# A fourth seven-product pair per matrix group, with seven sets of weight sums made during attention and parked in DRAM

## The chip, the cores and the metric

The kernel is one launch on one core of a Trainium2 chip. The metric is device time in microseconds. Before the change it is 1458.26 us (median of three runs, 1458.24 to 1458.92). The core's engines are named as in the profile: PE (matrix products), PEld (its weight loads, which overlap), DVE (elementwise work), ACT (casts, copies, activation functions), POOL (a little elementwise work, and some transfers) and SP (which here only issues transfers).

## The reference

One transformer-like block on x of 256 tokens by 2048. The parts that matter here, cut from the reference:

```
proj = x @ w_in[l]                       # split into q,k,v of two attentions, z, gate_a, gate_b, ...
o_a  = gated_delta_rule_chunked(...)     # a chunked linear attention, with convolution and norm, times silu(z)
o_b  = dsa_sparse_attention(...)         # a top-64 attention
merged = sigmoid(gate_a) * (o_a @ w_branch_a[l]) + sigmoid(gate_b) * (o_b @ w_branch_b[l])
x = layer_norm(ALPHA * x + merged @ w_out[l], ...)
h_gate, h_up = split(x @ w_ffn_in[l], 2)
x = layer_norm(ALPHA * x + (silu(h_gate) * h_up) @ w_ffn_out[l], ...)
```

All inputs are fp32 and the result must be near fp32.

## The kernel before, in words

**Products.** Every fp32 matrix is split into a high part (a cast by ACT, `hi`) and a low part (the difference, by DVE, `lo`). One product is then three matmuls, high by high, high by low and low by high (`mm3`, the lines L210, L211 and L212 of the profile). A chunk of weights is 128 rows by 1024 columns, 512 KB: SP loads it into `raw` (L84), ACT casts it (L86), DVE subtracts (L88).

**Pairs.** A large projection is worked in groups of 1024 columns. The 2048 rows are taken as eight pairs of chunks, q = 0 to 7, and a group adds its eight pairs up in PSUM. A plain pair (`plain_pair`) is eight products, 24 matmuls of 512 columns. A seven-product pair (`seven_pair`) treats the pair as a 2 by 2 block product in Winograd's way: seven products, 21 matmuls. It pays for the missing product with sums: of the weights (`sum13` and `sum24`, DVE, into tiles named `wt`, `f_wt`, `g_wt`), which are split by ACT and DVE too (`thi` and `tlo`), and of x (`x_form`, made once for each q). It also needs four more PSUM banks (`wbank`), which hold the sums that several results share; a short chain (`sums_chain`) adds them up behind the group's last seven-product pair. The two sets of four banks, `acc` and `aux`, change roles from group to group, so `wbank` of one group are the banks that the group before summed its result in, and they are free when DVE has read that result out (L1054 in the gates).

A pair whose weight sums were made ahead (`early_sums`, found in a `ready` table) needs only its first chunk and half of its second one in the usual way. For all others the sums stand right ahead of the pair, among the operations of that pair.

**Which pairs.** The tables GQ (four gate groups), ZQ (z), OQ (output projection) and FQ (ten feed-forward groups) name the pairs that use seven products, and GO and ZO the order of the pairs. Before, most groups have three (2, 4 and 6), the third gate group four.

**Order of work.** PE and SP run in the order in which the program is written. DVE, ACT and POOL are ordered by a scheduler from that program and from priorities. Side work stands in generators (`start`, `tick`): each pair ticks a clock twice, and a generator writes its next piece when its tick comes. So a transfer that such a generator issues on SP stands in SP's list at that place, between the loads of weights.

**Stages**, by the profile of before: first projections, convolution and both attentions (to about 330 us), z, two gate groups for `gate_b`, the product with w_branch_b, two gate groups for `gate_a`, the product with w_branch_a (to about 650), output projection and first layer norm (to about 760), two feed-forward groups in plain form, ten feed-forward groups with pairs (`wfg`, from about 800 to 1227), then the product with w_ffn_out and the last norm. A feed-forward group's result is finished by `hidden_chain`, which among others puts eight transposes (L1337) on PE.

Of the kernel before, what the change touches and what calls it, by code (L numbers as in the profile page):

```python
# [58 lines left out]
def block_kernel(ctx: ExitStack, tc: tile.TileContext, xT, x, cpack, onehot, relb, convw, alog, dtb, gnw,  # L59
# [96 lines left out]
    def join(dst, ps):  # L156
        t = p1.tile([P, S], F32, name="half2", tag="half2", bufs=2)
        nc.scalar.copy(t, ps[:, S:])
        nc.vector.tensor_add(dst, ps[:, :S], t)
# [174 lines left out]
    def T(name, shape, dtype=F32, tag=None):  # L334
        return p1.tile(shape, dtype, name=name, tag=tag or name)
# [140 lines left out]
    def conv_chain(c, pss, ev, dst, c0):  # L476
        pres = []
        for ps in pss:
            pre = p1.tile([P, S], F32, name="pre", tag="pre", bufs=2)
# [431 lines left out]
    for ch in (gates_chain, key_chain, query_chain, value_chain, index_chain, attend_chain, out_gate_chain):  # L911
        start(ch())

    conv_first(s_kT, pss)
    event("kc0")
# [25 lines left out]
    def z_chain():  # L941

        yield "v1"
        yield 1
        t0 = [rp.tile([P, 2, 1024], F32R, name=f"z_t{i}", tag=f"x1_{i}") for i in range(2)]
        wt = two("z_wt", F32, "ol_")
# [36 lines left out]
    def late_form(q):  # L983
        t = T(f"g_form{q}", [P, 2, 4, P], F32R, tag="s_rv")
        gates_form[q] = t[:, 0], t[:, 1]
        room = gates_home["wt"][1][0]
        x_form(q, gates_form[q], room[:, :512], room[:, 512:])

    def ga_chain(src, qs):
        for q in qs:  # L990
            yield from early_sums(src, q, home, ga_ready)
        event("gaready")

# [70 lines left out]
    def merged_chain(j):  # L1064
        yield 1 if j < 3 else 2
        for tb in range(NTB):
            with tc.high_priority(offset=LEAD):
                transposed_split(ga, j, tb)
            yield 1
        if 2 * j in OQ:  # L1070
            yield 1
            room = s_mn.rearrange("p a h d -> p (a h d)")
            x_form(2 * j, gates_form[2 * j], room[:, :512], room[:, 512:1024])
# [8 lines left out]
    def ga_rows():  # L1082
        if "a" not in g_rows:
            for tag in ("thi", "tlo"):
                gates_home[tag] = [0, gates_home[tag][1][:2]]
# [3 lines left out]
    z_ready, ga_ready = {}, {}  # L1089
    start(z_chain())  # L1090
# [12 lines left out]
    late_form(0)  # L1103
    start(ga_chain(wgt[2], (2, 4)))
    for j in range(4):
# [4 lines left out]
    for i in range(2):  # L1110
        gate_group(ga_rows, 2 + i)
    ga = ga_rows()
    need("oa")
    for j in range(4):
# [43 lines left out]

    def load_x():
        for tb in range(NTB):  # L1160
            x1[tb] = rp.tile([P, D], F32, name=f"x1_{tb}", tag=f"x1_{tb}")
            nc.gpsimd.dma_start(x1[tb], x[:, tb, :])

    bank = x_group(woa, OQ, ps_acc, ps_aux, gates_form, home,
                   lambda wbank: seven_chain(0, wbank, mnv.rearrange("p t d -> p (t d)")[:, 1024:1536]), {2: load_x})
    finish()
# [126 lines left out]
    hp2 = fh.enter_context(tc.tile_pool(name="hp2", bufs=1, side="left", reuse_waits="tile"))  # L1293
    for i in (5, 6):
        h_tile(hp2, i)

# [24 lines left out]
    for tb, ps in enumerate(block_xs([wfi[1, k] for k in range(8)], xh, xl)):
        start(h_chain(1, tb, gated(tb, ps), ps_acc))
# [44 lines left out]
    for i in range(1, NG + 1):  # L1367
# [6 lines left out]

        bank = x_group(wfg[i - 1], FQ[i - 1], std, shared, f_form, fhome, lambda wbank: sums_chain(places(), wbank))
        if i == NG:
# [260 lines left out]
```

## Time and profile before

| | |
|---|---|
| median of the runs | 1458.26 us |
| profiled execution | 1458.29 us |
| its span | 1456.5 us |
| PE busy | 1448.7 us (99%) |
| DVE busy | 1241.6 us (85%) |
| ACT busy | 802.6 us (55%) |
| POOL busy | 48.3 us (3%) |
| moved by transfers | 313.32 MB, mean 215 GB/s |
| granted TensorE clock | 1.0 in every stretch |

The span is the profiled execution without 1.8 us around it. Times of the traces below count from the span's start. An engine's busy share is a mean over stages; what a stage has left is read from the windows of that stage.

### The profile page before, as it was taken

What the parts mean: (1) busy time and instruction counts of PE and PEld (TensorE: products, weight loads), DVE (VectorE), ACT (ScalarE), POOL (GpSimd) and SP (SyncE); (2) the same over time, 40 slices, a digit from 0 to 9 for tenths busy, and PEclk for the clock granted to TensorE, in tenths of its full rate; (3) what the DMA queues carried; (4) which work ended last, traced back from release to release, by engine and by line L of the source; (5) the groups of instructions that cost most, each with busy time, mean ns of one, the idle gap of its engine ahead of it and who ended that gap; (6) DMA issues with size and microseconds to landing.
All of it is one profiled execution on the core that took longest, in us unless ns stands there. A gap on an engine that the chain in (4) does not pass through costs nothing.

```text
span 1456.5 us, 19507 instructions
## 1 busy us (share of the span) xinstructions
PE 1448.7 (99%) x7167; PEld 1218.8 (84%) x7167; DVE 1241.6 (85%) x1692; ACT 802.6 (55%) x993; POOL 48.3 (3%) x61
## 2 busy tenths in 40 slices
PE   9999999999999999999999999999999999999998
PEld 8888888888888888888888888888888888888887
DVE  6798985488699958879886899989999998989987
ACT  5765443347466645645535565656566565554552
POOL 0002010020000000000000000000000000000000
PEclk9999999999999999999999999999999999999999
DMA  8646575544556765556856667656666667887853
GB/s 294 195 157 196 178 185 172 172 162 153 174 182 222 239 211 189 192 192 231 296 178 221 227 236 245 210 206 206 228 204 212 216 216 248 310 340 263 330 202 117
DMA packets 94768, 313.32 MB, mean 215 GB/s; under 512 B 16896, under 2 KB 18088, under 8 KB 93904
## 3 DMA queue, kind: packets, MB, share of 16 engines
q1 hardware_dynamic: 83328, 293.25, 59.1%
q0 software_dynamic: 4160, 16.46, 3.6%
q10 hardware_dynamic: 7184, 2.36, 0.7%
q8 instruction: 56, 0.92, 0.2%
q14 instruction: 40, 0.33, 0.1%
HBM read 298.20 MB, written 13.83 MB: 214 GB/s over the span
## 4 chain that ended last, share of the span: by engine, by line
PE 98%; DMA 1%; DVE 0%; ACT 0%; SPq 0%; issue 0%; POOLq 0%; ACTq 0%; DVEq 0%
PE acc L211 11%; PE acc L210 11%; PE acc L212 11%; PE acc L148 10%; PE aux L210 10%; PE aux L212 10%; PE aux L211 10%; PE acc L151 5%; PE acc L168 4%; PE acc L170 4%; PE acc L169 3%; PE aux L168 1%; PE aux L170 1%; PE aux L169 1%; PE aux L723 1%; DMA raw<-in_win_dram 1%
## 5 line engine op out<-in xcount | busy, mean ns | idle before, releaser
L86 ACT CAST hi<-raw 128x1024 fp32r<-128x1024 f32 (+1 forms) x390 | 402.7, 1041 | 367.8 <-PE acc L148 88.2
L88 DVE TENSOR_TENSOR lo<-raw,hi 128x1024 fp32r<-128x1024 f32 (+1 forms) x390 | 470.7, 1216 | 129.2 <-ACT hi L86 126.1
L148 PE MATMUL acc<-X,hi 128*128 128x512 f32 x640 | 203.7, 400 | 0.0
L210 PE MATMUL acc<-hi,X 128*128 128x512 f32 x400 | 156.7, 392 | 0.0
L212 PE MATMUL acc<-hi,X 128*128 128x512 f32 x400 | 155.7, 389 | 0.0
L211 PE MATMUL acc<-lo,X 128*128 128x512 f32 x400 | 155.7, 389 | 0.0
L151 PEld LDWEIGHTS acc<-X,lo 128*128 128x128 f32 x640 | 120.2, 188 | 28.3
L210 PE MATMUL aux<-hi,X 128*128 128x512 f32 x336 | 131.3, 391 | 0.0
L212 PE MATMUL aux<-hi,X 128*128 128x512 f32 x336 | 130.8, 389 | 0.0
L211 PE MATMUL aux<-lo,X 128*128 128x512 f32 x336 | 130.7, 389 | 0.0
L151 PE MATMUL acc<-X,lo 128*128 128x256 f32 x640 | 126.0, 278 | 0.0
L148 PEld LDWEIGHTS acc<-X,hi 128*128 128x128 f32 x640 | 97.5, 189 | 2.0 <-ACT hi L86 0.7
L234 ACT CAST f_thi<-f_wt 128x1024 fp32r<-128x1024 f32 x58 | 61.1, 1053 | 52.4 <-DVE f_wt L244 30.8
L212 PEld LDWEIGHTS acc<-hi,X 128*128 128x128 f32 x400 | 75.1, 188 | 15.7
L210 PEld LDWEIGHTS acc<-hi,X 128*128 128x128 f32 x400 | 75.1, 188 | 15.3 <-ACT s_u L925 0.2
L211 PEld LDWEIGHTS acc<-lo,X 128*128 128x128 f32 x400 | 75.1, 188 | 15.2
L235 DVE TENSOR_TENSOR f_tlo<-f_wt,f_thi 128x1024 fp32r<-128x1024 f32 x58 | 70.2, 1221 | 6.2 <-ACT f_thi L234 6.0
L212 PEld LDWEIGHTS aux<-hi,X 128*128 128x128 f32 x336 | 63.1, 188 | 13.2
L211 PEld LDWEIGHTS aux<-lo,X 128*128 128x128 f32 x336 | 63.1, 188 | 13.0
L210 PEld LDWEIGHTS aux<-hi,X 128*128 128x128 f32 x336 | 63.1, 188 | 12.8
L168 PE MATMUL acc<-hi,X 128*128 128x512 f32 x160 | 64.3, 402 | 0.0
L234 ACT CAST thi<-wt 128x1024 fp32r<-128x1024 f32 x36 | 37.9, 1054 | 45.9 <-DVE wt L239 27.0
(593 smaller groups left out, 2961.5 us busy)
## 6 DMA issues: line engine op xcount, KB each, us to landing
raw<-in_wfg_dram SPq DMA_DIRECT2D x131, 512.0 KB, 4.1
raw<-in_wws_dram SPq DMA_DIRECT2D x80, 512.0 KB, 3.8
raw<-in_wfo_dram SPq DMA_DIRECT2D x70, 512.0 KB, 4.9
raw<-in_wgt_dram SPq DMA_DIRECT2D x51, 512.0 KB, 3.6
f_wraw<-in_wfg_dram SPq DMA_DIRECT2D x29, 512.0 KB, 5.9
raw<-in_win_dram SPq DMA_DIRECT2D x21, 512.0 KB, 3.7
wraw<-in_wfo_dram SPq DMA_DIRECT2D x18, 512.0 KB, 4.9
gt<-d_g SPq DMA_DIRECT2D x18, 512.0 KB, 6.5
```

Source lines behind the costliest of these rows:

```text
L86: nc.scalar.copy(hi, raw)
L88: nc.vector.tensor_sub(lo, raw, hi.bitcast(F32))
L148: nc.tensor.matmul(pss[c], hv[:, kk, cs[c]], X2[k // 4][:, k % 4], start=(k == 0), stop=False, skip_group_check=True)
L151: nc.tensor.matmul(pss[c][:, :S], lv[:, kk, cs[c]], xh[:, k, :], start=False, stop=(k == KT - 1), skip_group_check=True)
L168: nc.tensor.matmul(ps, xh, hv[:, kk], start=(k == 0), stop=False)
L169: nc.tensor.matmul(ps, xh, lv[:, kk], start=False, stop=False)
L170: nc.tensor.matmul(ps, xl, hv[:, kk], start=False, stop=(k == 2 * n - 1))
L210: nc.tensor.matmul(o, sh, hi, start=first, stop=False)
L211: nc.tensor.matmul(o, sh, lo, start=False, stop=False)
L212: nc.tensor.matmul(o, sl, hi, start=False, stop=last)
L234: nc.scalar.copy(hi, v)
L235: nc.vector.tensor_sub(lo, v, hi.bitcast(F32))
```

## The change

Ten pairs of the kind q = 0 become seven-product pairs: in the second and the fourth gate group, in the output projection, and in feed-forward groups 1 to 7.

- For the seven feed-forward groups the weight sums are made by a new generator, `kept_chain`, that starts with the attention generators. For each group it loads the two chunks into one tile (POOL, 1 MB), makes the four sums (DVE, four additions of 512 columns), splits them (ACT two casts, DVE two subtractions of 1024) and writes both parts to a DRAM tensor `d_s` (POOL, twice 1 MB). Its two tiles are those that held the first projection's small weights; z's early sums, which use the same room, are written only after the generator is through (`need("kept")`).
- In the feed-forward stage `kept_load` brings a set back: four SP loads of 512 KB into four tiles. The first set is loaded beside the second plain group, each next one from the pair q = 5 of the group before on. The tiles are single. The pairs run in the order FO, with the kept one fourth.
- In the two gate groups the new pair makes its sums in place, and comes second in the group; before, the first seven-product pair came third.
- In the output projection two pairs (0 and 2) have early sums, made beside the product with w_branch_a, and the order is OO.
- The sums of x for q = 0 (`late_form(0)`) move from behind the second gate group to a generator that is started ahead of the first one. They are made in tiles that attention leaves, and the scheduler puts them near the program's start. `f_forms_chain` makes a set for q = 0 too.
- To make room, the small tiles `half2` and `pre` become pieces of one tile, `load_x` comes in halves, and the space for POOL's transfer descriptors is set to 8192 bytes.

The diff, cut to its core:

```diff
-GQ = ((2, 4, 6), (2, 4, 6), (0, 2, 4, 6), (2, 4, 6))
-GO = (range(8), range(8), (1, 3, 2, 4, 5, 6, 0, 7), range(8))
+GQ = ((2, 4, 6), (0, 2, 4, 6), (0, 2, 4, 6), (0, 2, 4, 6))
+GO = (range(8), (1, 0, 3, 2, 5, 4, 6, 7), (1, 3, 2, 4, 5, 6, 0, 7), (1, 0, 3, 2, 5, 4, 6, 7))
+OO = (1, 3, 0, 2, 5, 4, 6, 7)
-OQ = (2, 4, 6)
+OQ = (0, 2, 4, 6)
-FQ = ((4, 6), *[(2, 4, 6)] * 9)
+KEPT = 7
+FQ = ((0, 4, 6), *[(0, 2, 4, 6)] * (KEPT - 1), *[(2, 4, 6)] * (10 - KEPT))
+FO = (1, 3, 2, 0, 4, 5, 6, 7)
...
+    d_s = dr.tile([KEPT, 2, P, 2, 1024], F32, name="d_s")
+    def kept_chain():
+        raw, hi = T("k_raw", [P, 2, 1024], tag="oh_"), T("k_hi", [P, 2, 1024], F32R, tag="ol_")
+        (r0, r1), (s0, s1) = ([raw[:, i, n * 512:n * 512 + 512] for n in range(2)] for i in range(2))
+        for m in range(KEPT):
+            nc.gpsimd.dma_start(raw, wfg[m, 0:2].rearrange("k p c -> p k c"))
+            yield 3
+            nc.vector.tensor_add(r0, r0, s1)
+            nc.vector.tensor_add(s1, r1, s1)
+            yield 1
+            nc.vector.tensor_add(r1, r0, r1)
+            nc.vector.tensor_add(s0, r1, s0)
+            yield 1
+            for i in range(2):
+                nc.scalar.copy(hi[:, i], raw[:, i])
+                nc.vector.tensor_sub(raw[:, i].bitcast(F32R), raw[:, i], hi[:, i].bitcast(F32))
+                yield 1
+            nc.gpsimd.dma_start(d_s[m, 0], hi.bitcast(F32))
+            nc.gpsimd.dma_start(d_s[m, 1], raw)
+            yield 4
+        event("kept")
...
+    def kept_load(m):
+        for i in range(2):
+            if m:
+                kept[i] = [hp2.tile([P, 1024], F32R, name="kept", tag=f"{hl}{5 + i}") for hl in ("hH", "hL")]
+            for j in range(2):
+                nc.sync.dma_start(kept[i][j].bitcast(F32), d_s[m, j, :, i])
+                yield 2
...
+        k_ready[0] = t1, t2, t3, t4
...
+        at = {5: lambda i=i: start(kept_load(i))} if i < KEPT else {}
+        bank = x_group(wfg[i - 1], FQ[i - 1], std, shared, f_form, fhome, lambda wbank: sums_chain(places(), wbank),
+                       at, FO, k_ready)
```

**Where instructions move: SP in the feed-forward groups.** One steady group of SP's list before, in which `f_wraw` with the `raw` behind it are the two loads of a seven-product pair, here of q = 2, 4 and 6:

```order
L273 DMA f_wraw<-in_wfg_dram 128x1024
L275 DMA raw<-in_wfg_dram 128x1024
L84 DMA raw<-in_wfg_dram 128x1024 x2
L273 DMA f_wraw<-in_wfg_dram 128x1024
L275 DMA raw<-in_wfg_dram 128x1024
L84 DMA raw<-in_wfg_dram 128x1024 x2
L273 DMA f_wraw<-in_wfg_dram 128x1024
L275 DMA raw<-in_wfg_dram 128x1024
L84 DMA raw<-in_wfg_dram 128x1024 x6
```

The same place after the change, from the pair q = 4 on:

```order
L276 DMA f_wraw<-in_wfg_dram 128x1024
L278 DMA raw<-in_wfg_dram 128x1024
L87 DMA raw<-in_wfg_dram 128x1024 x2
L1373 DMA kept<-d_s 128x1024
L276 DMA f_wraw<-in_wfg_dram 128x1024
L278 DMA raw<-in_wfg_dram 128x1024
L1373 DMA kept<-d_s 128x1024
L87 DMA raw<-in_wfg_dram 128x1024 x2
L1373 DMA kept<-d_s 128x1024
L87 DMA raw<-in_wfg_dram 128x1024 x2
L1373 DMA kept<-d_s 128x1024
```

The first of the four `kept` loads stands ahead of the two loads of q = 6, and waits until PE has read the tile's present contents, which it does in the group's own fourth pair.

**DVE from the first to the second gate group.** Before (L1008 to L1013 add up the shared banks of the first group, L1054 read its result out, the rest prepares the second group's pairs):

```order
L1008 TENSOR_TENSOR gb_4291<-gb_4291,acc 128x512
L1009 TENSOR_TENSOR gb_4290<-acc,gb_4291 128x512
L1012 TENSOR_TENSOR gb_4291<-gb_4291,acc 128x512
L1013 TENSOR_TENSOR gb_4291<-acc,gb_4291 128x512
L1054 TENSOR_TENSOR gb_4290<-aux,gb_4290 128x512
L88 TENSOR_TENSOR lo<-raw,hi 128x1024
L239 TENSOR_TENSOR g_wt<-g_wraw,raw 128x1024
L1054 TENSOR_TENSOR gb_4290<-aux,gb_4290 128x512
L243 TENSOR_TENSOR g_wt<-g_wt,g_wraw 128x512
```

and now (L1049 to L1054 are the former L1008 to L1013, L1095 the former L1054):

```order
L1049 TENSOR_TENSOR gb_4322<-gb_4322,acc 128x512
L242 TENSOR_TENSOR g_wt<-g_wraw,raw 128x1024
L1050 TENSOR_TENSOR gb_4321<-acc,gb_4322 128x512
L246 TENSOR_TENSOR g_wt<-g_wt,g_wraw 128x512
L1053 TENSOR_TENSOR gb_4322<-gb_4322,acc 128x512
L247 TENSOR_TENSOR g_wt<-g_wt,raw 128x512
L1054 TENSOR_TENSOR gb_4322<-acc,gb_4322 128x512
L238 TENSOR_TENSOR lo<-g_wraw,hi 128x1024
L238 TENSOR_TENSOR lo<-raw,hi 128x512
L238 TENSOR_TENSOR g_tlo<-g_wt,g_thi 128x1024 x2
L1095 TENSOR_TENSOR gb_4321<-aux,gb_4321 128x512
L91 TENSOR_TENSOR lo<-raw,hi 128x1024
```

The sums and splits of the second group's first seven-product pair now stand ahead of all four reads of the first group's result. Before, one read stood ahead of them, one among them, and two followed them (further down, not shown).

More of the change, by code (lines that the diff above doesn't have):

```diff
@@ L156, in join @@
     def join(dst, ps):
-        t = p1.tile([P, S], F32, name="half2", tag="half2", bufs=2)
+        t = pieces(1)
         nc.scalar.copy(t, ps[:, S:])
@@ L347, in block_kernel, with pieces @@
     s_sq = T("s_sq", [P, 1024])
+    s_pc = T("s_pc", [P, 1024])
+    T("s_x", [P, 2048])
+    turns = [0, 0]
+    def pieces(i):
+        turns[i] += 1
+        return s_pc[:, (2 * i + turns[i] % 2) * S:(2 * i + turns[i] % 2 + 1) * S]
     first_ = [T(n, [P, H * S], F32R, tag=t) for n, t in (("wsh", "oh_"), ("wsl", "ol_"))]
@@ L478, in conv_chain @@
         for ps in pss:
-            pre = p1.tile([P, S], F32, name="pre", tag="pre", bufs=2)
+            pre = pieces(0)
             join(pre, ps)
@@ L912, in block_kernel @@
         start(ch())
+    d_s = dr.tile([KEPT, 2, P, 2, 1024], F32, name="d_s")
[19 more added lines that the diff above has]
+        event("kept")
+    start(kept_chain())
     conv_first(s_kT, pss)
@@ L944, in z_chain @@
         yield 1
+        need("kept")
         t0 = [rp.tile([P, 2, 1024], F32R, name=f"z_t{i}", tag=f"x1_{i}") for i in range(2)]
@@ L983, in late_form, with early_chain, next_sets @@
     def late_form(q):
-        t = T(f"g_form{q}", [P, 2, 4, P], F32R, tag="s_rv")
+        t = T(f"g_form{q}", [P, 2, 4, P], F32R, tag="s_pc")
         gates_form[q] = t[:, 0], t[:, 1]
-        room = gates_home["wt"][1][0]
+        yield 3
+        room = T("f_room", [P, 1024], tag="s_x")
         x_form(q, gates_form[q], room[:, :512], room[:, 512:])
-    def ga_chain(src, qs):
+    def early_chain(src, qs, ready, ev):
         for q in qs:
-            yield from early_sums(src, q, home, ga_ready)
-        event("gaready")
+            yield from early_sums(src, q, home, ready)
+        event(ev)
+    def next_sets(*olds):
+        for tag, old in zip(("thi", "tlo"), olds):
+            e = gates_home[tag]
+            gates_home[tag] = [0, e[1][:2] + halves(two("h_" + old, F32R, old))[1]]
     def x_form(q, dst, x32, g):
@@ L1071, in merged_chain @@
             yield 1
-            room = s_mn.rearrange("p a h d -> p (a h d)")
+            room = wo_room
             x_form(2 * j, gates_form[2 * j], room[:, :512], room[:, 512:1024])
@@ L1097, in block_kernel @@
     gates_buffers()
+    start(late_form(0))
     for i in range(2):
@@ L1102, in block_kernel @@
         gates_home[tag][0] = 0
-    late_form(0)
-    start(ga_chain(wgt[2], (2, 4)))
+    start(early_chain(wgt[2], (2, 4), ga_ready, "gaready"))
     for j in range(4):
@@ L1112, in block_kernel @@
     ga = ga_rows()
+    next_sets("s_x", "s_rv")
+    wo_room = T("wo_room", [P, 2048], tag="s_mn")
+    start(early_chain(woa, (0, 2), wo_ready, "woready"))
     need("oa")
@@ L1293, in block_kernel @@
     hp2 = fh.enter_context(tc.tile_pool(name="hp2", bufs=1, side="left", reuse_waits="tile"))
-    for i in (5, 6):
-        h_tile(hp2, i)
+    kept = [[hp2.tile([P, 1024], F32R, name="kept", tag=f"{hl}{i}") for hl in ("hH", "hL")] for i in (5, 6)]
     f_home = {}
@@ L1318, in f_forms_chain @@
             x_form(q, f_form[q], fv(), fv())
+    k_ready = {}
+    def kept_load(m):
[5 more added lines that the diff above has]
+                yield 2
+        (t1, t2), (t4, t3) = ([tuple(t[:, n * 512:n * 512 + 512] for t in kept[i]) for n in range(2)]
+                              for i in range(2))
+        k_ready[0] = t1, t2, t3, t4
     start(f_forms_chain())
+    start(kept_load(0))
     for tb, ps in enumerate(block_xs([wfi[1, k] for k in range(8)], xh, xl)):
@@ L1373, in places @@
             return sums
-        bank = x_group(wfg[i - 1], FQ[i - 1], std, shared, f_form, fhome, lambda wbank: sums_chain(places(), wbank))
+        at = {5: lambda i=i: start(kept_load(i))} if i < KEPT else {}
+        bank = x_group(wfg[i - 1], FQ[i - 1], std, shared, f_form, fhome, lambda wbank: sums_chain(places(), wbank),
+                       at, FO, k_ready)
+        if i == KEPT:
+            for k in (5, 6):
+                h_tile(hp2, k)
         if i == NG:
```

20 lines of the change are left out of this document (11 added, 9 removed).

## The prediction

> **What bounds the kernel now.** I read the page's busy times and chain first, then what PE waited for, then the windows of DVE stage by stage.
>
> ```profile
> span 1456.5 us, 19507 instructions
> PE 1448.7 (99%) x7167; PEld 1218.8 (84%) x7167; DVE 1241.6 (85%) x1692; ACT 802.6 (55%) x993; POOL 48.3 (3%) x61
> PE 98%; DMA 1%; DVE 0%; ACT 0%; SPq 0%; issue 0%; POOLq 0%; ACTq 0%; DVEq 0%
> PE aux L407 <- DVE warm L403: 1.1, 1, 1.1
> PE acc L134 <- DVE lo L88: 1.1, 3, 0.6
> ```
>
> PE is busy for 99% of the span and makes 98% of the chain. Its two largest waits are 1.1 us each, both at the start. So time goes down only by matmuls that disappear, and comes back only as new waits of PE. The next two questions are what a matmul is worth, and how much room DVE has where it gets more to do.
>
> ```profile
> 858.63 0.39 PE L210 MATMUL aux<-hi,X 128*128 128x512 f32 x1
> 860.90 0.39 PE L211 MATMUL aux<-f_tlo,f_form 128*128 128x512 f32 x1
> ...
> 80.00:94.00 14.00, 14.00 (x89) 12.50 (x88) 14.00 (x27) 11.29 (x15) 0.77 (x3) 1.00 0.47 144
> 94.00:108.00 14.00, 14.00 (x91) 12.56 (x90) 13.74 (x57) 8.76 (x12) 0.20 (x1) 1.00 0.49 160
> 108.00:122.00 14.00, 14.00 (x85) 12.34 (x84) 10.97 (x23) 7.63 (x11) 5.08 (x2) 1.00 0.68 169
> 122.00:136.00 14.00, 14.00 (x82) 12.20 (x81) 11.04 (x31) 9.17 (x14) 0.16 (x1) 1.00 0.63 227
> ...
> 443.00:464.00 21.00, 21.00 (x94) 17.41 (x93) 20.07 (x23) 14.75 (x18) 0.00 (x0) 1.00 0.71 239
> 464.00:485.00 21.00, 21.00 (x94) 17.38 (x94) 18.43 (x24) 11.48 (x15) 0.00 (x0) 1.00 0.59 190
> 590.00:611.00 21.00, 21.00 (x95) 17.38 (x94) 17.41 (x19) 11.18 (x13) 0.00 (x0) 1.00 0.57 179
> 674.00:695.00 21.00, 21.00 (x94) 17.41 (x93) 20.93 (x27) 12.64 (x15) 0.00 (x0) 1.00 0.72 258
> 989.00:1010.00 21.00, 21.00 (x94) 17.41 (x93) 18.34 (x23) 11.19 (x13) 0.00 (x0) 1.00 0.72 237
> 1010.00:1031.00 21.00, 21.00 (x99) 17.47 (x98) 21.00 (x27) 14.26 (x19) 0.53 (x1) 1.00 0.52 184
> ```
>
> From the first to the last of the two matmuls there are ten steps in 2.27 us, so 0.227 us each, though each shows 0.39: they overlap. In the windows the third busy figure is DVE's. DVE has no idle time left at 80 to 94 us (14.00 of 14), about 3.5 of 42 us in the second gate group, and 2.7 of 42 in a feed-forward group.
>
> **What is removed.** Ten pairs go from 24 to 21 matmuls: 30 x 0.227 = 6.8 us. Nothing lies over these, so if PE waits no more than before, the profiled execution of 1458.29 becomes 1451.5. Everything below is what PE may wait for again.
>
> **The kept sums beside attention.** For DVE and ACT the prices are these:
>
> ```profile
> L88 DVE TENSOR_TENSOR lo<-raw,hi 128x1024 fp32r<-128x1024 f32 x381 | 464.5, 1228 | 124.4 <-ACT hi L86 121.4
> L235 DVE TENSOR_TENSOR lo<-raw,hi 128x512 fp32r<-128x512 f32 x62 | 42.5, 686 | 0.0
> 107.55 1.22 DVE L88 TENSOR_TENSOR lo<-raw,hi 128x1024 fp32r<-128x1024 f32 x1
> 113.72 0.39 PE L151 MATMUL acc<-X,lo 128*128 128x256 f32 x2
> 124.66 1.22 DVE L88 TENSOR_TENSOR lo<-raw,hi 128x1024 fp32r<-128x1024 f32 x1
> 128.53 0.39 PE L151 MATMUL acc<-X,lo 128*128 128x256 f32 x2
> x<-in_x_dram POOLq DMA_DIRECT2D x2, 1024.0 KB, 7.9
> ```
>
> Back to back the 1024 form takes about 1.13 us and the 512 form 0.60 (starts in the feed-forward rows below), so a set is 4 x 0.60 + 2 x 1.13 = 4.7 us of DVE, seven sets 33 us. Most of it lies in attention's idle DVE time. It doesn't where DVE is full: the second set's work falls at about 73 to 91 us by its place among neighbours that exist in both programs. The window ahead still takes some of it; I carry about 3.5 us of lateness past 94, and DVE is idle for 0.26 until 108 and 3.0 until 122. The low part made at 107.55 ends at 108.77 and is used at 113.72: 4.95 us of room, less the 3.5 and what of the third set comes before it, so 0 to 0.5 lost. The one at 124.66 ends at 125.88 and is used at 128.53, 2.65 of room, against about 3.5 - 3.0 left plus the third set's pieces in that place: 0 to 1.5. The other places have more room. POOL adds a chain of its own: it holds back each next load until the last set's writes have landed, and attention's reciprocal roots wait behind that in its queue. The seven sets lie between about 35 and 260 us, some 30 us apart, and a 1 MB transfer of POOL's landed after 7.9 us (the last row), so I count on cover there: write, load and 4.7 us of sums fit; without it, the next set's first sum holds DVE, in order, for as long as the load is late. In all 0 to 3; I take **0.6**, nearer the covered end because all but two of the places have over 3 us.
>
> x_form(0) near the start is five small operations more among the first chunks (0.69 + 4 x 0.29 = 1.9 us at most), next to PE's start-up waits of 1.1: 0 to 0.3, taken 0.1. It leaves the stage behind the second gate group, where DVE had no idle time, which helps there.
>
> **Gates and output projection.** A pair that makes its own sums costs DVE 1.13 + 1.13 + 0.60 + 1.13 + 2 x 0.60 + 1.13 = 6.3 us against 2.3 for a plain one: 4 more in each of two gate groups. The fourth has 3.6 idle in its middle half and more behind; the second about 3.5 of its 42, less 0.7 by which it shrinks. And its shared banks are wanted 5.44 us earlier:
>
> ```profile
> 439.40 0.68 DVE L1008 TENSOR_TENSOR gb<-gb,acc 128x512 f32<-128x512 f32 x1
> 442.72 0.69 DVE L1054 TENSOR_TENSOR gb<-aux,gb 128x512 f32<-128x512 f32 x1 [0.33 <-PE aux L212]
> 445.44 1.23 DVE L239 TENSOR_TENSOR g_wt<-g_wraw,raw 128x1024 f32<-128x1024 f32 x1 [0.89 <-DMA raw<-in_wgt_dram]
> 438.38 0.33 SPq L275 DMA_DIRECT2D raw<-in_wgt_dram  x1
> 444.56 0.39 PE L210 MATMUL acc<-hi,X 128*128 128x512 f32 x1
> 455.44 0.39 PE L210 MATMUL aux<-hi,X 128*128 128x512 f32 x1
> 567.83 0.69 DVE L1008 TENSOR_TENSOR ga<-ga,aux 128x512 f32<-128x512 f32 x1 [0.83 <-ACT ga L1006]
> ```
>
> The group begins at 444.56, the first shared bank was wanted at 455.44 and is now at 450.0, the fourth 2.0 later. I walk DVE's new list from 439.40: the sum can start at 440.3 if its rows have landed (their buffer comes free around 435.5 instead of 438), and seven operations up to the fourth bank's sum end at 444.4, two 1024 splits, a 512 and another 1024 at 448.4; the first read ends at 449.0, the fourth, with a low part between, at 451.9 (wanted by 453.4). Room about 1 us everywhere. The same walk from the last row's place, where the idle 0.83 takes most of the first sum, leaves the fourth group 0.6 to 1.3. So 0 if loads are on time; a load as late as the one above (7.1 us from 438.38 to 445.44) would cost about 1.5 in each group. With the lateness carried into the product behind the second group, 0 to 3; taken **0.3**. In the output projection the two early pairs take work out of a full stage (20.93 of 21) and the first shared bank is wanted third as before: 0.
>
> **Feed-forward: the kept loads on SP.** DVE gets 0.5 us less per group, so its share is no issue. What changes is SP's list. Before, the loads of q = 6 ran far ahead:
>
> ```profile
> 974.94 0.43 SPq L273 DMA_DIRECT2D f_wraw<-in_wfg_dram  x1
> 978.57 0.33 SPq L275 DMA_DIRECT2D raw<-in_wfg_dram  x1
> 986.82 1.22 DVE L239 TENSOR_TENSOR f_wt<-f_wraw,raw 128x1024 f32<-128x1024 f32 x1
> 994.44 1.23 DVE L235 TENSOR_TENSOR f_tlo<-f_wt,f_thi 128x1024 fp32r<-128x1024 f32 x1 [1.20 <-ACT f_thi L234]
> 996.02 0.39 PE L210 MATMUL acc<-hi,X 128*128 128x512 f32 x1
> 999.64 0.39 PE L211 MATMUL acc<-f_tlo,f_form 128*128 128x512 f32 x1
> f_wraw<-in_wfg_dram SPq DMA_DIRECT2D x29, 512.0 KB, 5.9
> raw<-in_wfg_dram SPq DMA_DIRECT2D x131, 512.0 KB, 4.1
> ```
>
> Call the start of q = 6 on PE Q (996.02 here). The two loads were issued at Q - 21.1 and Q - 17.5, the sum made at Q - 9.2, and the last low part, which ends at 995.67, was ready 4.0 us before its use at Q + 3.6. Now the `kept` load ahead of them waits for the end of the fourth pair, q = 0, which lies before q = 4 (4.76), q = 5 (5.44) and q = 6: Q - 10.4. So f_wraw goes out at about Q - 10.1 and raw at Q - 9.7; SP stands still for about 11 us, with the loads of q = 6, q = 7 and the next group's first pairs behind it. With 5.2 us for the one and 6.4 for the other in such a burst they land at Q - 4.9 and Q - 3.3. Then DVE, which has waited some 5 us: low part to Q - 2.7, sum to -1.6, 512 low part -1.0, half sum -0.4, low part of the first sum 0.8 (wanted at 2.3), half sum 1.4, one low part of q = 7 2.5, low part of the second sum 3.7, wanted at 3.6. That is just enough. With the medians' 4.1 us for raw, 2.2 of room; with the 7.1 of the gates' load, 0.8 lost. Six groups have such a load: 0 to 4.8, taken 0.2 each, **1.2**. DVE comes out about 3.7 us late of that place and meets little idle time afterwards (2.7 per group), so the transposes' inputs and the next second pair lose up to 1 now and then: **0.3**, with 0 to 2.
>
> [...]
>
> The traffic that the loads add, 2 MB less 0.25 per 41.7 us, is some 42 GB/s on 184 to 237, and is covered:
>
> ```profile
> 1346.00:1367.00 21.00, 21.00 (x95) 17.38 (x94) 20.27 (x22) 12.29 (x14) 2.08 (x4) 1.00 0.97 354
> ```
>
> Here 354 GB/s moved and PE stayed busy for 21.00 of 21. The small descriptor space, the halves of load_x and the moved tiles I take at 0; POOL has 97% of its time free.
>
> **Sum.** 1458.29 - 6.8 + 0.6 + 0.1 + 0.3 + 1.2 + 0.3 = 1454.0. The profiled execution is 0.03 above the median, which changes nothing.
>
> **Rivals.**
> - *Nothing waits:* 1451.5 to 1452.2. For it: the walks end with room, if small; against it: four places with 1 us or less.
> - *The kept load starves q = 6.* One mechanism, SP's standstill, decides alone. Each us by which `raw` lands after Q - 3.2 costs PE one us in each of six groups. At 1.1 us (landing 7.5 after its issue) the gain is all but gone with the other terms: 1458.6, no change. Slower than 1461.2 takes 1.6 or more, a landing at 8 us: the four transfers, q = 7's and POOL's would have to share. At 9 us it is 1458.29 - 6.8 + 1.3 + 6 x 2.6 = 1468. For it: the burst of six loads after 11 us of silence and the 7.1 above; against it: the 5.9 median, in the same stage.
> - *DVE in attention:* the sets come late, by POOL's chain or by lateness that adds up over the full windows, and PE waits once for each set in three or four places, 1 to 1.5 us each: 1454.0 - 0.6 + 4 to 5 = 1457.4 to 1458.4, no change.
>
> [...]
>
> **Chances.** A change of 0.2% (2.9 us) is about what can be told here. The sum as worked out, 1452.2 to 1455.3: 0.48. Nothing waits: 0.14. Standstill to no change 0.18, to slower 0.10. Attention 0.10, no change. Together faster 0.62, no change 0.28, slower 0.10. I predict 1454.0, with 1452.2 to 1456 as its own range; eight in ten lie within 1451.4 to 1459.0.
>
> **What would show it.** In the profile after: PE busy near 1442 and its waits, by releaser. If I am right, PE's waits grow by 1 to 4 us, the most on L235's successor (f_tlo, L238) once per feed-forward group, and f_wraw of q = 6 goes out about 10 us before its pair, right behind a kept load. DVE's idle time before sum13 (`f_wt`) grows by about 5 us in six groups, released by a transfer. If PE waits for lo (L91) between 105 and 135 us, attention was underrated. If PE waits on L1095 at 448 to 454 or 576 to 582, the gates were. The forecast is wrong if PE's waits exceed 5 us in all, or if the kept loads' standstill isn't there.

## The result and the profile after

The changed kernel takes 1479.44 us (median of four runs, 1477.17 to 1482.98). The kernel before, run beside it, takes 1458.25 (four runs, 1457.68 to 1458.92). The ratio is 1.0146, with a 95% interval of 1.0133 to 1.0158: slower by 21 us, where 1454.0 was forecast and 1459.0 was the end of the range.

The page of the changed kernel, its span, busy times and chain:

```profile
span 1478.1 us, 19641 instructions
PE 1454.1 (98%) x7137; PEld 1217.4 (82%) x7137; DVE 1281.3 (87%) x1761; ACT 818.8 (55%) x1019; POOL 63.8 (4%) x84
PE 74%; DVE 13%; DMA 8%; issue 3%; ACT 2%; SPq 0%; POOLq 0%; ACTq 0%; DVEq 0%
```

PE does 30 matmuls fewer (7137 for 7167), but it is no longer the whole chain: 98% has become 74%, and 21% lies on DVE and transfers. The list of what PE waited for (us in total, times, longest):

```profile
PE acc L154 <- DVE lo L91: 5.9, 4, 2.8
PE aux L613 <- ACT s_t L619: 3.1, 1, 3.1
PE aux L214 <- DVE h_s_rv L238: 1.5, 1, 1.5
PE aux L214 <- DVE f_tlo L238: 1.5, 3, 0.8
PE acc L214 <- DVE f_tlo L238: 1.3, 2, 0.8
...
PE aux L213 <- DVE v L1054: 0.8, 1, 0.8
```

L154 and L613 stand in attention, h_s_rv in the output projection, f_tlo and v in the feed-forward stage. Over all of the program PE's waits come to 19.5 us, against 3.5 before. To put a price on each place, I matched every matmul of a changed kernel to the same matmul of the kernel before and subtracted the times. The differences by stage, for the changed kernel and for four experiments told below (worked out from the profiled executions; minus is gained; each row holds what was gained or lost within that stage; "late load" is the kept load one pair later, "two tiles" the second form of that experiment):

```
us gained or lost in           changed  work only  late load  two tiles  four groups
start (to 60 us)                 +1.2     -0.1       -0.2       +0.7        +0.3
attention, 60 to 136             +9.6     +1.1       +9.8        0.0         0.0
attention, 136 to 206            +1.2     +0.3       +1.0        0.0         0.0
attention, 206 to 262            +6.6     +0.4       +3.7       +7.4        +0.6
262 to 440                        0.0     +0.2        0.0       +0.2        +0.3
two gate groups                  -1.4     -1.4       -1.3       -1.3        -1.3
output projection                +1.9     +2.0       +2.1       -0.7        -0.6
feed-forward groups              +2.5     +2.8       -4.8       -4.8        -2.7
```

A group whose new pair costs nothing else gains 0.68: 3 matmuls of 0.227. The gates show just that, twice. The changed kernel loses 17.4 in attention, 2.5 around the gain of 0.7 in the projection, and 7.3 around the gain of 4.8 (7 x 0.68) in the feed-forward groups.

**Attention, first place.** DVE's timeline at the second set (start, duration, operation; L932 is a set's first sum, L564 attention's own; the bracket is the idle time before an instruction and what ended it), then POOL's (L943 writes a set's low part, L930 loads the next set):

```profile
79.92 0.69 DVE L932 TENSOR_TENSOR k_raw<-k_raw 128x512 f32<-128x512 f32 x1 [6.78 <-DMA k_raw<-in_wfg_dram]
...
84.98 1.28 DVE L564 TENSOR_TENSOR s_e<-aux,gc 128x512 f32<-128x512 f32 x2
```

```profile
62.86 0.55 POOL L943 DMA_DIRECT2D d_s<-k_raw  x1 [4.23 <-DVE k_raw L940]
69.64 0.72 POOL L930 DMA_DIRECT2D k_raw<-in_wfg_dram  x1 [6.23 <-DMA d_s<-k_raw]
```

POOL can load the second set into the one tile only when the first set's write has landed, 6.2 us after POOL itself was free. The load then takes 10.3 us, from 69.64 to 79.92. DVE reached the first sum at 73.1 and stood there 6.78 us, with attention's own work behind it. Nothing of it shows on PE at once: PE has work until 89, and then waits for a low part at 90.90, 108.77 and 123.01. Three transfers were in flight together: in the windows from 62 to 68 us the DMA engines were busy all the time (1.01 to 1.04), and up to 76 for nine tenths of it or more (0.90 to 1.02). In the load's last 4 us they were not (0.68 of 76 to 78, 0.15 of 78 to 80); why it still had not landed is not shown.

```profile
64.00:66.00 2.00, 2.00 (x13) 1.76 (x12) 0.51 (x1) 1.99 (x4) 0.00 (x0) 1.00 1.02 422
...
74.00:76.00 2.00, 2.00 (x13) 1.77 (x12) 0.00 (x0) 1.90 (x5) 0.00 (x0) 1.00 0.97 322
```

The columns are the stretch, its length, busy times of PE, PEld, DVE, ACT and POOL, the granted clock, the DMA engines' busy share and GB/s. From 74 to 76 DVE does nothing. Afterwards it has no slack in which to catch up: from 80 to 124 us it waits only once more, for 0.9 us, and PE's three waits fall in this stretch.

The same stall of DVE costs nothing elsewhere. The seventh set's first sum waits too, 5.76 us, and PE stays full:

```profile
272.41 0.69 DVE L932 TENSOR_TENSOR k_raw<-k_raw 128x512 f32<-128x512 f32 x1 [5.76 <-DMA k_raw<-in_wfg_dram]
```

```profile
262.00:270.00 8.00, 8.00 (x70) 6.94 (x70) 2.45 (x2) 3.28 (x4) 0.72 (x1) 1.00 0.91 325
270.00:278.00 8.00, 8.00 (x53) 6.80 (x51) 5.45 (x9) 1.84 (x4) 0.00 (x0) 1.00 0.19 57
```

There DVE is busy for only 7.9 of 16 us; at 80 to 94 the kernel before had no idle time on it at all (14.00 of 14 in the prediction's windows).

**Attention, second place.** A piece of the chain, then POOL's timeline (s_bm is a gather of many small rows, eight transfers that attention needs):

```profile
228.76 12.06 DMA raw<-in_wws_dram
240.92 1.04 ACT hi L89
241.97 0.38 ACT s_t L619
```

```profile
212.61 0.53 POOL L943 DMA_DIRECT2D d_s<-k_raw  x1 [7.55 <-DVE sc L811]
219.80 0.71 POOL L930 DMA_DIRECT2D k_raw<-in_wfg_dram  x1 [6.66 <-DMA d_s<-k_raw]
220.50 3.73 POOL L825 DMA_DIRECT2D s_bm<-d_tab  x7
```

Here it is a weight load of SP's that is late: 12 us after its issue, where such loads took 3.8 in the median before. On ACT the small copy s_t stands behind that load's cast (240.92, then 241.97), so it is late too, and PE waits 3.1 us for it. Beside the load, POOL moves a 1 MB set and the gather; from 226 to 242 us the DMA engines were busy all the time (1.01 to 1.05 in windows of 4 us).

**Output projection.** POOL's x loads, SP's load of the early pair's second chunk, and DVE's sum:

```profile
686.72 1.17 POOL L1207 DMA_DIRECT2D x<-in_x_dram  x2 [337.22 <-PE aux L1102]
688.12 0.33 SPq L278 DMA_DIRECT2D raw<-in_woa_dram  x1
696.18 1.22 DVE L242 TENSOR_TENSOR g_wt<-g_wraw,raw 128x1024 f32<-128x1024 f32 x1 [4.52 <-DMA raw<-in_woa_dram]
```

The load lands 8 us after its issue and DVE stands for 4.5, ahead of two pairs with early sums; PE waits at 709.76 and 714.98.

**Feed-forward.** SP's timeline around a kept load, and DVE's up to the late low part:

```profile
920.55 0.33 SPq L1373 DMA_DIRECT2D kept<-d_s  x1
920.93 0.43 SPq L276 DMA_DIRECT2D f_wraw<-in_wfg_dram  x1
```

```profile
928.63 1.22 DVE L242 TENSOR_TENSOR f_wt<-f_wraw,raw 128x1024 f32<-128x1024 f32 x1
931.05 1.23 DVE L238 TENSOR_TENSOR f_tlo<-f_wt,f_thi 128x1024 fp32r<-128x1024 f32 x1
933.47 1.23 DVE L91 TENSOR_TENSOR lo<-raw,hi 128x1024 fp32r<-128x1024 f32 x1 [0.59 <-ACT hi L89]
934.61 1.22 DVE L238 TENSOR_TENSOR f_tlo<-f_wt,f_thi 128x1024 fp32r<-128x1024 f32 x1
```

```profile
935.88 0.50 PE L214 MATMUL acc<-f_tlo,f_form 128*128 128x512 f32 x1 [0.84 <-DVE f_tlo L238]
```

This is the standstill of the forecast, in its place and order. The idle time it makes stands on ACT, as its wait for f_wraw:

```profile
ACT hi L237 <- DMA f_wraw<-in_wfg_dram: 31.6, 6, 6.5
```

### The profile page after: what moved, and what is told of

The parts are those of the page before. It is cut to its first block, busy times and chain, and to the rows that moved or that the text cites. A ratio compares the mean times of both kernels' runs of the same rounds, so it can differ in the third digit from the quotient of the medians.

```text
span 1478.1 us, 19641 instructions
## 1 busy us (share of the span) xinstructions
PE 1454.1 (98%) x7137; PEld 1217.4 (82%) x7137; DVE 1281.3 (87%) x1761; ACT 818.8 (55%) x1019; POOL 63.8 (4%) x84
## 4 chain that ended last, share of the span: by engine, by line
PE 74%; DVE 13%; DMA 8%; issue 3%; ACT 2%; SPq 0%; POOLq 0%; ACTq 0%; DVEq 0%
PE acc L214 9%; PE acc L215 9%; PE acc L213 8%; PE aux L214 8%; PE aux L215 8%; PE aux L213 8%; PE acc L151 4%; PE acc L173 3%; PE acc L171 3%; PE acc L172 3%; DVE lo L91 3%; DMA raw<-in_wws_dram 2%; PE acc L154 2%; DMA f_wraw<-in_wfg_dram 1%; PE aux L171 1%
## 5 line engine op out<-in xcount | busy, mean ns | idle before, releaser
L89 ACT CAST hi<-raw 128x1024 fp32r<-128x1024 f32 (+1 forms) x388 | 396.0, 1031 | 338.8 <-PE acc L215 68.6
L91 DVE TENSOR_TENSOR lo<-raw,hi 128x1024 fp32r<-128x1024 f32 (+1 forms) x388 | 462.6, 1203 | 95.8 <-ACT hi L89 94.0
L154 PEld LDWEIGHTS acc<-X,lo 128*128 128x128 f32 x640 | 121.4, 191 | 37.5 <-DVE lo L91 9.3
L213 PE MATMUL acc<-hi,X 128*128 128x512 f32 x370 | 145.2, 392 | 0.0
L215 PE MATMUL acc<-hi,X 128*128 128x512 f32 x370 | 144.2, 390 | 0.0
L214 PE MATMUL acc<-lo,X 128*128 128x512 f32 x370 | 144.0, 389 | 0.0
L154 PE MATMUL acc<-X,lo 128*128 128x256 f32 x640 | 128.5, 283 | 6.0 <-DVE lo L91 5.9
L213 PE MATMUL aux<-hi,X 128*128 128x512 f32 x306 | 119.8, 392 | 1.1 <-DVE v L1054 0.8
L214 PE MATMUL aux<-lo,X 128*128 128x512 f32 x306 | 119.2, 390 | 0.4 <-DVE lo L238 0.4
L215 PE MATMUL aux<-hi,X 128*128 128x512 f32 x306 | 119.2, 389 | 0.0
L215 PEld LDWEIGHTS acc<-hi,X 128*128 128x128 f32 x370 | 69.5, 188 | 14.7
L213 PEld LDWEIGHTS acc<-hi,X 128*128 128x128 f32 x370 | 69.5, 188 | 14.1 <-ACT s_u L959 0.2
L214 PEld LDWEIGHTS acc<-lo,X 128*128 128x128 f32 x370 | 69.5, 188 | 14.1
L238 DVE TENSOR_TENSOR f_tlo<-f_wt,f_thi 128x1024 fp32r<-128x1024 f32 x58 | 70.4, 1220 | 1.7 <-ACT f_thi L237 1.5
L213 PEld LDWEIGHTS aux<-hi,X 128*128 128x128 f32 x306 | 57.4, 188 | 13.6 <-DVE v L1054 1.2
L214 PEld LDWEIGHTS aux<-lo,X 128*128 128x128 f32 x306 | 57.5, 188 | 12.5 <-DVE lo L238 0.9
L215 PEld LDWEIGHTS aux<-hi,X 128*128 128x128 f32 x306 | 57.4, 188 | 12.0
L171 PE MATMUL acc<-hi,X 128*128 128x512 f32 x160 | 64.3, 402 | 0.0
```

The costliest lines, as they stand in the source:

```text
L89: nc.scalar.copy(hi, raw)
L91: nc.vector.tensor_sub(lo, raw, hi.bitcast(F32))
L154: nc.tensor.matmul(pss[c][:, :S], lv[:, kk, cs[c]], xh[:, k, :], start=False, stop=(k == KT - 1), skip_group_check=True)
L171: nc.tensor.matmul(ps, xh, hv[:, kk], start=(k == 0), stop=False)
L213: nc.tensor.matmul(o, sh, hi, start=first, stop=False)
L214: nc.tensor.matmul(o, sh, lo, start=False, stop=False)
```

## The experiments

My first theory after the result had three independent parts: in attention DVE, in order, is held by a load that came late (and not by its own 33 us of work); in the projection the x loads collide with the early pair's loads; in the feed-forward stage the kept load stands ahead of q = 6's loads in SP's list. Rivals: DVE's added work itself; the added transfers as such.

**Gates and projection alone.** No sums made ahead, the feed-forward groups as before:

```diff
-KEPT = 7
+KEPT = 0
-    start(kept_chain())
-    start(kept_load(0))
```

> Only the gates and the output projection have their fourth pair; nothing is made beside attention or kept, and the feed-forward groups are as before. If the changed kernel's ledger by stage adds up (start +1.1, attention +17.5, gates -1.4, output projection -0.7 +2.5, feed-forward -4.8 +7.3), this gives 1458.25 + 1.1 - 1.4 - 0.7 + 2.5 = 1459.8. If the output projection's 2.5 us are an echo of the lateness that attention left, they are gone and it gives 1457.3.

Measured 1459.22 (ten runs) beside 1458.49: ratio 1.0004 [0.9994, 1.0014], the first of the two forecasts: the projection's loss is no echo of attention's. The gates gain 0.68 each; the projection gives 2.3 back around its 0.68, and PE's largest wait is the 1.5 us for h_s_rv, as in the changed kernel.

**The same with x loaded by SP**, late in the stage, instead of by POOL beside the early pair's loads:

```diff
-            nc.gpsimd.dma_start(x1[tb][:, cs], x[:, tb, cs])
+            nc.sync.dma_start(x1[tb][:, cs], x[:, tb, cs])
-                   ... {0: load_x}, OO, wo_ready)
+                   ... {7: load_x}, OO, wo_ready)
```

> As x1_gates_proj, with x loaded by SP behind the last non-ready seven-product pair. If POOL's x loads beside the early pairs made PE wait in the output projection, the 2.3 us lost there fall to 0.3 or less: 1456.4 to 1457.0. If DVE's order in that stage did, they stay: 1459.

Measured 1456.55 (ten runs, 1455.16 to 1460.32) beside 1458.08: ratio 0.999 [0.9981, 1.0000]. The wait for h_s_rv is gone and the projection gains a clean 0.68. So what the projection lost hung on the place and queue of the x loads, not on the early pairs' work; which of the two, place or queue, was not separated.

**The chain's transfers alone:** each set is loaded and written back, without sums and splits.

> The chain beside attention only loads and writes; the sums, casts and subtractions are left out (what is kept is then the plain weights). If late weight loads cost the time (SP's loads share the engines with POOL's), attention still loses 10 us or more: 1472 to 1479. If DVE's work costs it, or DVE's standstill at the sums' load, attention loses 3 at most: 1461 to 1465.

Measured 1474.83 (one run); 13.9 us lost in attention. It looks like a verdict for the transfers, but it does not separate them from POOL's order. Nothing paced POOL any more, its transfers ran back to back, and two small pieces of attention's own work were queued behind them: a reciprocal root (`rk`), which POOL did at 119.14 in the changed kernel, and the clearing of a tile (s_e, L679 on POOL), for which DVE then stood 9.96 us:

```profile
124.20 0.55 POOL L935 DMA_DIRECT2D d_s<-k_raw  x1 [10.02 <-DMA k_raw<-in_wfg_dram]
...
125.40 3.20 POOL L473 TENSOR_TENSOR rk<-ssk,half 128x16 f32<-128x16 f32 x1
143.31 0.16 DVE L682 TENSOR_TENSOR s_e<-s_e 128x2 f32<-128x2 f32 x1 [9.96 <-POOL s_e L679]
```

Nearly all of its loss lies between 114 and 136 us (in the times of the kernel before). What follows is only that a wait of POOL's can cost as much by this other way.

**The chain's work alone:** all sums and splits stay, but only the first set is loaded and written, so later sets wait for nothing.

```diff
-            nc.gpsimd.dma_start(raw, wfg[m, 0:2].rearrange("k p c -> p k c"))
+            if not m:
+                nc.gpsimd.dma_start(raw, wfg[m, 0:2].rearrange("k p c -> p k c"))
```

> The chain beside attention does all of its sums, casts and subtractions, but only the first of the seven sets is loaded and written; the others work on what lies there, and the feed-forward groups all read the first set. If DVE's work costs the time, attention still loses 14 us or more: 1475 or more. If the transfers do it, as late weight loads or as DVE's standstill at the sums' load, it loses 1 to 4: 1461 to 1466.

Measured 1463.63 (one run). Attention loses 1.8 in place of 17.4. DVE's rows at the second set (the lines stand one further down here, so L933 is a set's first sum):

```profile
71.81 0.68 DVE L933 TENSOR_TENSOR k_raw<-k_raw 128x512 f32<-128x512 f32 x1
...
77.80 1.29 DVE L564 TENSOR_TENSOR s_e<-aux,gc 128x512 f32<-128x512 f32 x2 [0.26 <-PE aux L563]
```

The sum starts without a wait, and attention's L564 at 77.80 in place of 84.98. So DVE's work for seven sets costs at most 1.8 us; the forecast's price for it was right. This run takes away the transfers and the standstill together; which of the two counts is left to the run with two tiles. The projection and the feed-forward stage lose as in the changed kernel.

**Kept load one pair later,** behind the loads of q = 6 in SP's list; the rest is the changed kernel:

```diff
-        at = {5: lambda i=i: start(kept_load(i))} if i < KEPT else {}
+        at = {6: lambda i=i: start(kept_load(i))} if i < KEPT else {}
```

> As the changed kernel, but each kept load starts one pair later, so that it stands behind the two loads of q = 6 in SP's list. If SP's standstill ahead of these loads makes the 7.3 us lost in the feed-forward groups, 5 of them or more are gone, and f_wraw of q = 6 goes out 15 us or more before its pair: about 1473 to 1475. If the kept bytes themselves (2 MB more per group) make them, the loss stays: 1478 to 1481.

Measured 1468.93 (one run), below the 1473 to 1475 expected. The feed-forward groups gain 4.75, which is 7 x 0.68: nothing is lost any more. No f_tlo and no v is left among PE's larger waits:

```profile
PE acc L154 <- DVE lo L91: 6.5, 4, 4.7
PE aux L613 <- ACT s_t L619: 1.5, 1, 1.5
PE aux L214 <- DVE h_s_rv L238: 1.5, 1, 1.5
```

So the place in SP's list was the whole cause there, with the waits for v as a consequence. Attention still loses 14.5. That is 2.9 less than in the changed kernel, and the start costs 1.4 less, though the edit touches neither; the changed kernel's own four runs spread over 5.8 us, so single runs are read here by stage and for differences larger than that of a stage left alone.

**Two set tiles.** With the late kept load and x by SP, each set is loaded a set ahead, into a second tile (that of `s_x`). Its first use must wait until s_x's old content is done with. In the first form I made that wait with a small copy on DVE that reads the first set:

```diff
+        nc.vector.tensor_copy(s_x[:, :1], raws[0][:, 0, :1])
+        raws.append(T("k_raw", [P, 2, 1024], tag="s_x"))
...
+            if m + 1 < KEPT:
+                load(m + 1)
             nc.vector.tensor_add(r0, r0, s1)
```

> All seven sets beside attention, with the later kept load of x4_late_load, x loaded by SP behind the last non-ready seven-product pair of the output projection instead of by POOL, and a second tile for the chain's load: each set is loaded a whole set ahead, so that DVE's sums need not wait for a load and the load not for the last set's writes. Bytes and DVE work are the same. If DVE's standstill at k_raw (13.9 us in the changed kernel) costs attention its time, its loss falls from 14.3 to 5 or less: 1453 to 1458. If the transfers themselves, which make SP's weight loads late, cost it, the loss stays at 9 or more: 1462 to 1467. In the output projection the 2.5 us should go, if POOL's x loads made the pair's second load late.

Measured 1464.07 (one run), and the copy had the very fault that it was to cure:

```profile
46.37 0.15 DVE L934 COPY s_x<-k_raw 128x1 f32<-128x1 f32 x1 [6.25 <-DMA k_raw<-in_wfg_dram]
```

DVE stood 6.25 us for it, and 4.8 us were lost at about 50 to 62. This repeats the mechanism in another place. Another 8.4 us followed up to 262, so the loss did not fall to the 5 expected. In the second form the copy reads a tile of attention that is long there, some steps later:

```diff
-        nc.vector.tensor_copy(s_x[:, :1], raws[0][:, 0, :1])
+        yield 6
+        nc.vector.tensor_copy(s_x[:, :1], s_kT[:, 0, :1])
```

> As x4_late_load, with the second tile of x5_double, but the first load into it waits for a result of the first convolution instead of being waited for by DVE (that wait cost x5_double 4.4 us before 60 us); x is loaded by POOL again. If DVE's standstill at the sums' load made 6 of attention's 14.3 us, as the difference of the two kernels says, 8 to 9 are left: 1462 to 1464. If it made nothing, 12 to 14 are left: 1466 to 1469.

Measured 1459.95 (one run). The kernel as it ran loads x by SP, unlike what the expectation says ("by POOL again"), which accounts for about 2.5 us of the distance to the 1462 to 1464 expected. Where the changed kernel loses 10.8 between 60 and 206 us, this one loses nothing, with the same sums and the same bytes. DVE's waits for a set fell from 13.9 us to 1.1 (L943 is a set's first sum here):

```profile
DVE k_raw L943 <- DMA k_raw<-in_wfg_dram: 1.1, 1, 1.1
```

```profile
114.00:136.00 22.00, 22.00 (x131) 19.24 (x131) 19.29 (x38) 13.09 (x19) 2.00 (x2) 1.00 0.72 213
...
220.00:240.00 20.00, 16.77 (x99) 14.24 (x99) 15.70 (x36) 7.42 (x11) 1.26 (x2) 0.83 0.87 342
```

What is left, 7.4 us, all lies between 206 and 240: the second place, where the two tiles change nothing.

**Four groups instead of seven.** Is that second place due to the sets' transfers that run there, or to something that earlier sets leave behind? With four sets the last write is out by 190 us, ahead of the gather:

```diff
-KEPT = 7
+KEPT = 4
```

> The second set tile kept, first load into it gated (as in the run with two set tiles), but only four groups have a kept pair, so the last set is written by about 190 us, before the gather of s_bm at 208 us; kept loads behind q6's loads, x loaded by SP. Matmuls away: two gate groups, the projection and four groups, 7 x 0.68 = 4.8 us. Theory 1 (what was left in attention with two set tiles, some 7 us, all between 206 and 240 us, is the fifth and sixth sets' 1 MB transfers beside the gather and the weight loads): less than 1 us is lost in attention, 1458.3 - 4.8 + 0.7 = 1454.2, faster than before and than gates and projection alone (1456.6). Theory 2 (the sets ahead of 190 us, by what they move in POOL's order or in the weight queue, cause the late stall too): it stays, some 5 to 7 us between 206 and 240, 1459 to 1460.5. Theory 3 (the four sets' work and transfers ahead of 206 us cost in sum what they did with one tile): 1462 or more.

Measured 1455.58 (eleven runs, 1454.90 to 1457.62) beside 1458.36: ratio 0.998 [0.9971, 0.9989]. The second place costs 0.6 in place of 7.4, and PE's waits, 3.3 us in all, lie at the start and the end of the program but for this one:

```profile
PE aux L613 <- ACT s_t L619: 0.3, 1, 0.3
```

So sets that are in flight at 206 to 240 us cause it, the first theory of the three. The median lies 1.4 over the 1454.2 expected; of that the table shows 0.3 at the start and 0.3 between 330 and 360, and the profiled execution, at 1455.02, was itself 0.6 under the median. This is the best version I found: 2.8 us, or 0.2%, faster than the kernel before, with seven pairs changed (two in the gates, one in the projection, four kept). What the four kept pairs add to that is not shown by the times: gates and projection alone, with x by SP, were 1.5 us faster than the kernel before, and the two intervals overlap. The table has their 2.7 us, in the feed-forward groups.

**Sets behind attention's full stretches.** The other way to keep out of both places: start the sets at about 262 us, in other tiles, with the sums of x for q = 0 (`late_form(0)`, which take those tiles next) waiting for them; for four, three and two groups.

> Four sets only, for feed-forward groups 1 to 4, made in other tiles and later, behind the last projection that attention waits for (from about 262 us on to the first gate group), where DVE and the transfers have more room; later kept load and x by SP as in x5_double. If it is where and with what they collide that makes sets dear, and not the sets, these four cost 0 to 2 us: 1458.4 - 1.4 - 0.7 - 2.7 + 0 to 2 = 1453.6 to 1455.6. If each set costs some 2.5 us wherever it stands (17.5 for seven): 1463.

Measured 1471.34 (four runs): ratio 1.0091 [1.0074, 1.0108], slower than either expectation. Attention up to 330 us loses 0.1, as expected, but 3.7 go between 330 and 360 and 11.4 between 410 and 500, where the gates' inputs wait for the chain (the first line, at 463.65; the second is the wait at 361.10):

```profile
PE acc L213 <- ACT g_form L204: 4.7, 1, 4.7
PE acc L213 <- ACT s_u L961: 3.3, 1, 3.3
```

> As x10_late2 with three sets. The third lies beside z, where the third set of x7_late4 went with 3.7 us of waiting at 361 us. If that comes back it costs more than the 0.7 that it brings: 1457 to 1458. If the fourth set pushed it there: 1454.

> As x7_late4 with two sets, for feed-forward groups 1 and 2. Their chain should be through near 335 us, ahead of z and of the sums of x that waited for it in x7_late4. If the place is what counts, the sets cost 0 to 0.5 us: 1458.1 - 1.4 - 0.7 - 1.4 + 0 to 0.5 = 1454.6 to 1455.5, below both kernels. If each set costs 2.5 us: 1459.6.

With three, 1460.40 (eleven runs), ratio 1.0012 [1.0003, 1.0021]; with two, 1463.43 (five runs), ratio 1.0033 [1.0020, 1.0046]; both slower than expected. The gates' inputs no longer wait (with three sets one gate group still gains nothing), but 5.3 and 9.1 us go between 330 and 360, which I had not expected. The windows there, of the kernel before and then of the one with two late sets:

```profile
326.00:362.00 36.00, 36.00 (x177) 30.26 (x176) 33.21 (x57) 25.85 (x56) 4.63 (x2) 1.00 0.44 148
```

```profile
326.00:362.00 36.00, 32.11 (x150) 25.56 (x148) 34.77 (x59) 25.07 (x54) 6.54 (x6) 1.00 0.57 196
```

DVE had 2.8 us of 36 to spare there, and PE now waits for what DVE and ACT make (s_u, lo). That the added work is late there is argued from these windows. Both runs wait 3.3 us for s_u; the one with two sets has 2.8 us more, for lo. Ahead of that its DVE stands 2.29 us for the second set's load (at 322.61), which the run with three does not, and then

```profile
342.23 0.69 DVE L1042 TENSOR_TENSOR f_room<-X 128x512 f32<-128x512 f32 x1 [1.21 <-DMA d_s<-k_raw]
```

for the last set's write, ahead of the first of the sums of x. With three sets these come later, behind this stretch. By these rows it is the same mechanism once more, DVE standing for a transfer where it has little slack, and the 2.8 us are most of the 3.8 by which two sets lose more; no run takes it away to show it.

## Why the prediction was wrong, step by step

- **What is removed (30 x 0.227 = 6.8): right.** Every group whose new pair is clean gains 0.68, in all runs.
- **Kept sums beside attention (0.6, at most 3): the step that failed.** 17.4 us. The costs of DVE's work were right, at most 1.8 by the run with work alone. What failed is "I count on cover there: write, load and 4.7 us of sums fit". The sets lie some 30 us apart on average, but the first two do not: the first set's low part was made by 62.6 and DVE reached the second set's first sum at 73.1, 10.5 us later. The write's landing and the load together took 17 (62.86 to 79.92), on DMA engines that were nine tenths busy or more up to 76. I named the consequence, "the next set's first sum holds DVE, in order", and then priced the term from rooms of 2.65 and 4.95 us as if that could not happen; 6.78 us of standstill uses both up. The two-tile run shows it, with the same bytes: no standstill, no loss between 60 and 206.
- **A part of that term I did not see:** weight loads of attention are themselves late beside a set's transfers and the gather (one took 12.06 us where 3.8 is the median before, with the DMA engines at 1.01 to 1.05). 6.6 of the 17.4. The run with four groups shows it by its absence: 0.6 lost there, and its weight loads from 205 to 245 us took 4.4 in the median, where the second form of the two tiles has 6.7.
- **The rival on DVE in attention** had the right mechanism, "the sets come late, by POOL's chain", but as an addition of 4 to 5 us with 0.10. The waits alone are 9.7 us in this stage (5.9, 3.1 and 0.7 at L91, L619 and L608); the granted clock, below, accounts for up to 5 more, and the last 2 to 3 are not broken down.
- **Start (0.1):** 1.2 in the changed kernel, but -1.1 to +0.7 in the experiments that have the same work; no cost of the change can be told from that.
- **Gates (0.3): right,** 0. The walk's rooms of about 1 us held.
- **Output projection (0): wrong,** 2.5. I looked at DVE's room and the order of banks, and took "the halves of load_x" at 0 without asking what else loads at that moment. Loading x elsewhere removed it.
- **Feed-forward (1.2 + 0.3): right mechanism, wrong size,** 7.3. The walk's 5.2 and 6.4 us for the two loads of q = 6 were an estimate of mine; here ACT's casts of them began 5.5 and 6.9 us after the issues (926.41 after 920.93, 928.33 after 921.45). In the group above q = 6 starts on PE at 931.24 (Q). The walk had the sum end at Q - 1.6, the first low part at Q + 0.8 and the half sum at Q + 1.4; measured are -1.4, +1.0 and +1.6. Then DVE meets an idle 0.59, because ACT casts q = 7's chunk late, having waited 1.37 us for its load, and the last low part ends at Q + 4.6 where 3.7 was worked out and 3.6 wanted: PE stands 0.84, against 0.2 taken for a group. ACT and the load of q = 7 were missing in that walk, and the lateness of DVE cost another 1.7 in one group where PE's matmuls wait until DVE has read out the shared banks (the v rows). The sum for the rival beside it was a little low, too: 1451.5 + 1.3 + 6 x 1.1 is 1459.4, not 1458.6.
- **Signs to look for:** waits for lo between 105 and 135, named as the sign of an underrated attention, came (108.77 and 123.01). The idle time before the feed-forward sums stood one step earlier than named: ACT waited for the load (31.6 us in six waits), and DVE for ACT ahead of the low part (L238, 23.1 us in eight waits, 3.0 in two before). PE was busy for 1454.1 us, not near 1442, and its waits of 19.5 us are far over the 5 named as the sign of a wrong forecast.

Added up, the profiled execution (1479.84) lies 25.8 us over the sum: 16.8 from attention, 5.8 from the feed-forward stage, 2.5 from the projection and 1.1 from the start, less 0.3 from the gates.

## What to carry to other kernels

Price a moved load by the two places it lies between in the waiting engine's own list, not by the mean distance of the loop: write, landing and load of one buffer form a chain, and here the closest pair of rounds decided (10.5 us apart, where the chain took 17). DVE's wait for a transfer cost nothing where DVE had slack (5.76 us for 0, at 7.9 busy of 16) and 9.6 us where it had none (6.78 us of wait, ahead of a stretch with 14.00 busy of 14 before the change), so load one buffer ahead or put the round where the engine idles. And ask of each new bulk transfer which small or urgent one shares its stretch: a load list's order (7.3 us, by one line) and the moment of an unrelated load (2.5 us) weighed more here than any engine's added work.

## What the runs showed of the hardware

The granted clock fell behind three short idle times of PE, of 1.74, 2.82 and 3.06 us. Windows of the changed kernel:

```profile
88.00:92.00 4.00, 2.26 (x14) 1.65 (x13) 4.00 (x7) 3.56 (x4) 0.00 (x0) 1.00 0.12 15
92.00:96.00 4.00, 4.00 (x18) 3.61 (x18) 4.00 (x5) 3.97 (x6) 0.10 (x1) 0.58 0.63 217
96.00:100.00 4.00, 4.00 (x27) 3.57 (x27) 3.93 (x12) 3.99 (x6) 0.68 (x3) 1.00 0.15 46
...
122.70:126.10 3.40, 3.09 (x10) 2.70 (x11) 3.40 (x6) 1.37 (x4) 2.61 (x1) 0.50 0.86 176
...
242.20:245.60 3.40, 3.21 (x12) 2.82 (x13) 3.40 (x10) 2.09 (x5) 0.00 (x0) 0.50 0.35 143
```

After 1.74 us without a matmul, up to 90.90, the four microseconds from 92 on ran at 0.58, with 18 matmuls started in place of the 27 of the next four: as an estimate from these rows about 1.3 us more lost. So that wait of PE cost nearly twice its own length. The waits of 2.8 us before 123.01 and of 3.1 us before 242.39 each ran into such a stretch, at 0.50. As an estimate from these windows (4 us at 0.58 and twice 3.4 us at 0.50, 1.7 us lost in each), the lower clock cost up to 5 us of attention's 17.4, beside the waits themselves.

The length of the wait alone did not decide it. With four late sets PE stood 3.3 us before 361.10, and the clock stayed at 1.00 in the 4 us behind it; with three it stood 3.3 us before 361.17, and the clock fell to 0.65 (first the run with four, then that with three):

```profile
361.00:365.00 4.00, 3.90 (x21) 3.35 (x22) 4.00 (x9) 2.10 (x4) 0.00 (x0) 1.00 0.46 171
361.00:365.00 4.00, 3.83 (x15) 3.34 (x16) 3.77 (x9) 2.17 (x4) 0.00 (x0) 0.65 0.43 160
```

What decided it there, these runs do not show.
